# Part of the first MLP product as seven half-size products, with weight sums made by adding DMAs

## The chip, the cores and the metric

The kernel runs on one core of a Trainium2 chip, as one program launched once. The metric is the device time of that program in microseconds (us); smaller is better. TensorE does the matrix products (PE in the profile, with PEld for its weight loads), VectorE the two-operand arithmetic (DVE), ScalarE the copies, casts and functions (ACT), GpSimd some helpers (POOL), and SyncE asks for most of the transfers (SP). The profile calls the sequencers that issue DMAs SPq, ACTq and POOLq.

## The reference

A two-layer encoder on 512 tokens of width 1024. Layer 0 has an attention mixer, layer 1 a retention mixer; each is followed by an MLP with 4096 hidden units. Only the MLP is touched in what it computes:

```python
def _rmsnorm(x, g):
    xf = x.astype(jnp.float32)
    y = xf * lax.rsqrt(jnp.mean(xf * xf, axis=-1, keepdims=True) + RMS_EPS)
    return (y * g.astype(jnp.float32)).astype(x.dtype)

def _mlp(x, norm_g, w1, w2):
    h = _rmsnorm(x, norm_g)
    return jnp.square(jax.nn.relu(h @ w1)) @ w2

def reference(x, ...):
    for layer in range(DEPTH):          # DEPTH = 2
        ...
        x = x + _mlp(x, mlp_norm[layer], w_mlp_in[layer], w_mlp_out[layer])
    return x
```

Here `w1` is 1024 x 4096 and `w2` 4096 x 1024, all in float32.

## The kernel before

**Layout.** The residual lies transposed in SBUF: `xT[d]` holds features 128d to 128d+127 on the partitions and the 512 tokens in a row. `Norm.add` splits each tile, times the gain, into a rounded part and a rest (`xh`, `xl`, of type float32r); the row factor of the norm, `rb` (`norm.rows`), is applied after the product, since it is one number per token. Weights are split in the same way by `load_w`: one DMA on SP brings 512 KB into a `wraw` tile of 128 x 1024 (three buffers), ScalarE writes the rounded part `whi` (line 157), VectorE the rest `wlo` (line 158), two buffers each. A product of two such numbers is three matmuls: hi x hi, hi x lo, lo x hi.

**One projection.** `proj_a` makes 256 output columns for all 512 tokens: for each of 8 row tiles k and each half m of the columns three matmuls with a 128 x 128 weight and a 128 x 512 moving operand (lines 176 to 178), 48 in all, into two PSUM banks (`acc`, four buffers; `aux` is a second group of four). Then `evac` is called for each bank.

**The MLP.** `mlp` runs over four quarters q of the hidden units. In each it calls `proj_a` four times for the first product (c = 0 to 3, 1024 columns of `w1`), and then four times for the second (`w2`, 8 row tiles of the quarter's hidden units, added into `xT` at line 1043). The last quarter of layer 1 uses `store` and `proj_b` in place of the second. In this text a **unit** is 512 columns of the first product, two calls of `proj_a`; there are 8 units in a layer, two in a quarter. The evacuation of one bank (lines 1029 to 1033) is a chain: VectorE `max(ps, 0) * rb`, ScalarE square, ScalarE cast to `hh`, VectorE `hl = h - hh`.

**Order.** The Python order gives priorities; a scheduler at build time then places the instructions of each engine in the order in which it thinks they become ready, and `high_priority` moves the weight splits ahead. On the chip each engine runs its list in that order and waits at semaphores. A tile of a pool with n buffers can be written again when every reader of the tile n turns before it is done; a load that needs it waits on its queue till then.

Besides the MLP the change touches small tiles of the two mixers (`rstd`, `ssq`, `rs`, `lg`, `gn` and others), the `ones` constants and the eight idle matmuls at the start (line 83), `rstd_c` in `cols`, and the tag of the output tile `o` in `store`.

Of the kernel before, what the change touches and what calls it, by code (L numbers as in the profile page):

```python
# [9 lines left out]
F32 = mybir.dt.float32  # L10
F32R = mybir.dt.float32r
AF = mybir.ActivationFunctionType
ALU = mybir.AluOpType
# [19 lines left out]
def hybrid_encoder_kernel(  # L33
# [40 lines left out]
    ones = consts.tile([P, P], F32, name="ones")  # L74
    V.memset(ones, 1.0)
# [6 lines left out]
    for _ in range(8):  # L82
        mm(idle[:, :P], ones, ones, start=True, stop=True)
    ones_r = consts.tile([P, P], F32R, name="ones_r")
    V.tensor_copy(ones_r, ones)
    isl = consts.tile([P, 16], F32, name="isl")
# [7 lines left out]
    V.tensor_scalar(nsink, hb[:, 0:8], -1.0, None, op0=ALU.mult)  # L94

# [245 lines left out]
    def cols(row):  # L341
# [6 lines left out]
        r = stat.tile([P, 16], F32, tag="rstd_c", name="rstd_c")  # L348
        V.tensor_copy(r[:, 0:8], pc[:, 0:8])
        return r  # L350


    def even_mixer(next_norm):
        es = ExitStack()
        pool = es.enter_context(tc.tile_pool(name="even", bufs=1))
        xg = new_xg()
# [43 lines left out]
        rstd = pool.tile([P, 16], F32, name="rstd")[:, :NB]  # L400

        def token_norms():
            ssq = pool.tile([P, 4, NB], F32, name="ssq")
# [14 lines left out]
            v = pool.tile([P, 16], F32, name="ssv")[:, :NB]  # L418
            V.tensor_scalar(v, ssq[:, 0], 1.0 / D, RMS_EPS, op0=ALU.mult, op1=ALU.add)
            rsqrt_small(rstd, v, NB, pool)  # L420
# [5 lines left out]
        class HeadNorm:  # L426
# [5 lines left out]
            def __init__(self, raw, dsts, extra=None):  # L432
# [3 lines left out]
                self.ss = pool.tile([P, NB, 6], F32, tag="ss", bufs=2, name="ss")  # L436
# [10 lines left out]
            def finish(self, order):  # L447
                nh, extra = self.nh, self.extra
                self.rs = pool.tile([P, NB, nh], F32, tag=f"rs{nh}", bufs=2, name="rs")
                v = pool.tile([P, NB, nh], F32, tag=f"sv{nh}", bufs=2, name="sv")  # L450
# [4 lines left out]
                rsqrt_small(flat(self.rs), flat(v), NB * nh, pool)  # L455
# [132 lines left out]
        def small(tag):  # L588
            return pool.tile([P, 4], F32, tag=tag, bufs=4, name=tag)
# [381 lines left out]
    def store(w, hid, pool):  # L971
# [17 lines left out]
        for half in range(2):  # L989

            def ev(t, ps):
                o = pool.tile([P, S], F32, tag="o", bufs=3, name="o")
# [17 lines left out]

    def mlp(layer, norm, on_final, last=False):
        with tc.tile_pool(name=f"mlp{layer}", bufs=1) as pool:
            rb = None
            for q in range(4):
                hid = [
                    (
                        pool.tile([P, S], F32R, tag=f"hh{k}", name="hh"),
                        pool.tile([P, S], F32R, tag=f"hl{k}", name="hl"),
                    )
                    for k in range(8)  # L1020
                ]
                for c in range(4):
# [27 lines left out]
    def odd_mixer(norm, next_norm):  # L1050
# [69 lines left out]
        class Quarter:  # L1120


            def __init__(self, qt):
                self.qt = qt
# [256 lines left out]
```

## Time and profile before

| what | value |
|---|---|
| median of 3 runs | 1368.46 us (1367.3 to 1368.81) |
| the profiled execution, its own time | 1366.27 us |
| its span in the profile | 1364.5 us |
| granted TensorE clock, mean | 0.999 |
| HBM read | 120.43 MB |

The profile is of one execution. Its span runs from the first to the last instruction that it shows; 1.77 us lie around it. Busy times are those of each engine; matmuls overlap, so the time that one takes is longer than the distance to the next one, and it is the distance that counts. The chain that ended last is followed back from the last instruction: at each step it names the instruction that was waited for.

### The profile page before, as it was taken

Reading aid. Unit: us, or ns where it says so; the run is one execution under the profiler, and the core shown is the slowest. Engines: PE = TensorE matmul, PEld = TensorE weight load, DVE = VectorE, ACT = ScalarE, POOL = GpSimd, SP = SyncE. Lnnn points to the kernel's source line nnn. Section 1 sums busy time; section 2 is a strip of 40 time slices with the busy share of each in tenths; the row PEclk is TensorE's granted clock in tenths of the full one; section 3 lists DMA queues with packets and bytes.
Section 4 is the critical chain, followed back from the end, with each engine's and each line's share of the span. In section 5 each row is a group of like instructions: output and inputs, shape, how many; then the busy total and the mean of one; then the engine's idle time right before and its main releaser. Section 6 shows DMA issues by size and latency. Waiting matters only on the chain.

```text
span 1364.5 us, 16240 instructions
## 1 busy us (share of the span) xinstructions
PE 1346.2 (99%) x6218; PEld 1118.4 (82%) x6218; DVE 767.7 (56%) x1228; ACT 591.8 (43%) x1008; POOL 68.1 (5%) x80
## 2 busy tenths in 40 slices
PE   8999999999999999999999999999999999999998
PEld 7889887788888888888888888888888888888887
DVE  6788887634434434576758448547575344343433
ACT  4788775422313323344734445435354133241331
POOL 0223333000000000000000000000000000000000
PEclk9999999999999999999999999999999999999999
DMA  5322322323233233332231331331332333223322
GB/s 168 88 79 84 98 63 85 108 93 93 94 104 96 93 93 105 96 106 62 78 95 47 97 102 47 93 96 53 99 93 93 93 102 99 93 93 96 105 87 84
DMA packets 129502, 124.64 MB, mean 91 GB/s; under 512 B 9472, under 2 KB 122128, under 8 KB 129424
## 3 DMA queue, kind: packets, MB, share of 16 engines
q1 hardware_dynamic: 123648, 120.21, 28.3%
q10 hardware_dynamic: 5744, 3.37, 0.9%
q8 instruction: 49, 0.80, 0.2%
q14 instruction: 29, 0.24, 0.1%
q0 software_dynamic: 32, 0.01, 0.0%
HBM read 120.43 MB, written 3.15 MB: 91 GB/s over the span
## 4 chain that ended last, share of the span: by engine, by line
PE 91%; DVE 4%; ACT 2%; DMA 1%; issue 1%; POOL 0%; ACTq 0%; SPq 0%; DVEq 0%
PE acc L176 22%; PE acc L178 22%; PE acc L177 22%; PE acc L252 4%; PE acc L251 4%; PE acc L253 4%; PE aux L1202 1%; PE aux L1204 1%; PE aux L1203 1%; PE acc L200 1%; PE acc L202 1%; PE acc L201 1%; DVE wlo L158 1%; PE acc L229 1%; PE acc L227 1%
## 5 line engine op out<-in xcount | busy, mean ns | idle before, releaser
L157 ACT CAST whi<-wraw 128x1024 fp32r<-128x1024 f32 (+2 forms) x227 | 230.1, 1014 | 640.1 <-PE acc L177 531.5
L158 DVE TENSOR_TENSOR wlo<-wraw,whi 128x1024 fp32r<-128x1024 f32 (+2 forms) x218 | 261.1, 1198 | 293.3 <-ACT whi L157 292.0
L176 PE MATMUL acc<-xh,whi 128*128 128x512 f32 x784 | 305.4, 390 | 1.4 <-DVE xT L848 1.4
L177 PE MATMUL acc<-xl,whi 128*128 128x512 f32 x784 | 305.3, 389 | 0.3 <-DVE xl L298 0.3
L178 PE MATMUL acc<-xh,wlo 128*128 128x512 f32 x784 | 305.3, 389 | 0.0
L176 PE MATMUL acc<-hh,whi 128*128 128x512 f32 x448 | 176.5, 394 | 0.0
L178 PE MATMUL acc<-hh,wlo 128*128 128x512 f32 x448 | 175.6, 392 | 0.0
L177 PE MATMUL acc<-hl,whi 128*128 128x512 f32 x448 | 173.9, 388 | 0.0
L176 PEld LDWEIGHTS acc<-xh,whi 128*128 128x128 f32 x784 | 147.1, 188 | 32.6 <-DVE xT L848 1.8
L177 PEld LDWEIGHTS acc<-xl,whi 128*128 128x128 f32 x784 | 147.2, 188 | 31.6 <-DVE xl L298 1.0
L178 PEld LDWEIGHTS acc<-xh,wlo 128*128 128x128 f32 x784 | 147.1, 188 | 31.0 <-DVE wlo L158 0.2
L178 PEld LDWEIGHTS acc<-hh,wlo 128*128 128x128 f32 x448 | 84.1, 188 | 19.7
L177 PEld LDWEIGHTS acc<-hl,whi 128*128 128x128 f32 x448 | 84.1, 188 | 18.8
L176 PEld LDWEIGHTS acc<-hh,whi 128*128 128x128 f32 x448 | 84.2, 188 | 16.8
L1029 DVE SCALAR_TENSOR_TENSOR t<-acc,rstd_b 128x512 f32<-128x512 f32 x64 | 43.7, 692 | 77.1 <-PE acc L178 77.0
L1043 DVE TENSOR_TENSOR xT<-xT,acc 128x512 f32<-128x512 f32 x56 | 38.5, 688 | 76.1 <-PE acc L178 76.1
L251 PE MATMUL acc<-whi,xh 128*128 128x512 f32 x160 | 63.4, 396 | 0.0
L252 PE MATMUL acc<-wlo,xh 128*128 128x512 f32 x160 | 62.9, 393 | 0.2 <-DVE wlo L149 0.2
L253 PE MATMUL acc<-whi,xl 128*128 128x512 f32 x160 | 62.3, 390 | 0.0
L201 PE MATMUL acc<-wlo,xh 128*128 128x384 f32 (+1 forms) x160 | 52.6, 329 | 0.0
L200 PE MATMUL acc<-whi,xh 128*128 128x384 f32 (+1 forms) x160 | 52.6, 331 | 0.0
L202 PE MATMUL acc<-whi,xl 128*128 128x384 f32 (+1 forms) x160 | 52.1, 327 | 0.0
(231 smaller groups left out, 1915.4 us busy)
## 6 DMA issues: line engine op xcount, KB each, us to landing
wraw<-in_w_mlp_in_dram SPq DMA_DIRECT2D x64, 512.0 KB
wraw<-in_w_mlp_out_dram SPq DMA_DIRECT2D x64, 512.0 KB
wraw<-in_w_in_o_dram SPq DMA_DIRECT2D x48, 512.0 KB
wraw<-in_w_out_o_dram SPq DMA_DIRECT2D x16, 512.0 KB
wraw<-in_w_in_e_dram SPq DMA_DIRECT2D x48, 128.0 KB
wraw<-in_w_in_e_dram SPq DMA_DIRECT2D x12, 256.0 KB
wraw<-in_w_out_e_dram SPq DMA_DIRECT2D x4, 512.0 KB
wraw<-in_w_out_e_dram SPq DMA_DIRECT2D x8, 256.0 KB
```

Of the source, the lines that this page charges most:

```text
L157: nc.scalar.copy(hu, used)
L158: eng.tensor_tensor(lu, used, hu.bitcast(F32), op=ALU.subtract)
L176: mm(ps[m], hi[:, k % 4, cs], xh, start=k == 0, stop=False)
L177: mm(ps[m], hi[:, k % 4, cs], xl, start=False, stop=False)
L178: mm(ps[m], lo[:, k % 4, cs], xh, start=False, stop=k == nk - 1)
L200: mm(o, lh, hi[:, k, :ncols], start=kb + k == 0, stop=False)
L201: mm(o, lh, lo[:, k, :ncols], start=False, stop=False)
L202: mm(o, ll, hi[:, k, :ncols], start=False, stop=kb + k == KT - 1)
L251: mm(o, lh, hi[:, k, :ncols], start=kb + k == 0, stop=False)
L252: mm(o, lh, lo[:, k, :ncols], start=False, stop=False)
L253: mm(o, ll, hi[:, k, :ncols], start=False, stop=kb + k == KT - 1)
L1029: V.scalar_tensor_tensor(t, ps, 0.0, rb, op0=ALU.max, op1=ALU.mult)
```

## The change

In both layers units 2 to 7 of the first product are made by a class `Seven`, and units 0 and 1 as before, with `proj_a`. `Seven` cuts the 512 columns of a unit into two halves of 256, the 1024 rows of the weight into even and odd row tiles, and the 512 tokens into two halves of 256. That gives 2 x 2 blocks on both sides, and the four result blocks come from seven products of blocks instead of eight, in Winograd's form of Strassen's scheme. Each of the seven is 4 row tiles x 2 column tiles x 3 matmuls, with a 128 x 256 moving operand.

- **Input side.** `combine` makes for each pair of row tiles four sums of blocks (U1, U2, T3, T4) and splits them, four times per layer, in units 0 and 1; they serve all six units.
- **Weight side.** A unit needs seven 128 x 1024 blocks: A11, A12, A22 as loaded; S1 = A21 + A22 and S3 = A21 + A11, each loaded by a DMA on SP and completed by a second DMA on GpSimd that adds into the tile (the signs of the scheme are taken up elsewhere, so that all are sums); S2 = S1 + A11 and S4 = S2 + A12 by VectorE, S4 in S2's place. Three tiles each for loaded blocks (`sraw`), sums (`ssum`), rounded parts (`shi`) and rests (`slo`).
- **Order.** The blocks are split two products ahead of their use (`prepare`). The loads of the next unit stand in the program ahead of the fourth product of this one.
- **Output side.** The seven products run through three banks, `a` (four of the products, accumulating), `b` (one) and `c` (two). ScalarE copies partial results out (`keep`), VectorE adds (`add`), and `evac` ends each of the four result blocks with the same chain of four instructions; two blocks are negated and use `min` for `max`.
- **Around it.** The hidden units lie in tiles of 128 x 2 x 512, `t` and `h` become one tile squared in place, the small tiles of the mixers move into pools of their own, `ones` is written as float32r and used for the idle matmuls, `rstd_c` becomes a constant tile, and a filler of 80 words per partition is added.

```diff
-    ones = consts.tile([P, P], F32, name="ones")
-    V.memset(ones, 1.0)
+    ones_r = consts.tile([P, P], F32R, name="ones_r")
+    V.memset(ones_r[:].bitcast(F32), 1.0)
...
-        mm(idle[:, :P], ones, ones, start=True, stop=True)
-    ones_r = consts.tile([P, P], F32R, name="ones_r")
-    V.tensor_copy(ones_r, ones)
+        mm(idle[:, :P], ones_r, ones_r, start=True, stop=True)
...
+    class Seven:
+        BLOCKS = ("A11", "A12", "S2", "S1", "S3", "S4", "A22")
+        INPUTS = ("B11", "B21", "U2", "U1", "T3", "B22", "T4")
...
+        def combine(self, i):
+            pool, norm = self.pool, self.norm
+            y = []
+            for m in range(2):
+                d = 2 * i + m
+                t = pool.tile([P, S], F32, tag="s", bufs=5, name="y")
+                act(t, xT[d], AF.Copy, scale=gv[:, norm.vec + d : norm.vec + d + 1])
+                y.append(t)
+            b11, b12 = y[0][:, :256], y[0][:, 256:]
+            b21, b22 = y[1][:, :256], y[1][:, 256:]
+            c = pool.tile([P, 4, 256], F32, tag="slo", bufs=3, name="c")
+            V.tensor_tensor(c[:, 0], b11, b12, op=ALU.subtract)
+            V.scalar_tensor_tensor(c[:, 1], c[:, 0], -1.0, b22, op0=ALU.mult, op1=ALU.subtract)
+            V.tensor_tensor(c[:, 2], b22, b12, op=ALU.subtract)
+            V.scalar_tensor_tensor(c[:, 3], c[:, 1], -1.0, b21, op0=ALU.mult, op1=ALU.subtract)
+            h = pool.tile([P, 4, 256], F32R, tag=f"uh{i}", name="uh")
+            l = pool.tile([P, 4, 256], F32R, tag=f"ul{i}", name="ul")
+            nc.scalar.copy(h, c)
+            V.tensor_tensor(l, c, h[:].bitcast(F32), op=ALU.subtract)
...
+        def load(self, u, names=("S1", "S3", "A11", "A12", "A22")):
+            r = self.raw.setdefault(u, {})
+            for name in names:
+                tag = "ssum" if name[0] == "S" else "sraw"
+                r[name] = self.pool.tile([P, 4, 256], F32, tag=tag, bufs=3, name=tag)
+                if name[0] == "S":
+                    nc.sync.dma_start(r[name], self.source(u, "A21"))
+                    second = self.source(u, "A22" if name == "S1" else "A11")
+                    G.dma_start(r[name], second, accum_op=ALU.add)
+                else:
+                    nc.sync.dma_start(r[name], self.source(u, name))
+
+        def split(self, u, j):
+            name, r = self.BLOCKS[j], self.raw[u]
+            if name == "S2":
+                r[name] = self.pool.tile([P, 4, 256], F32, tag="ssum", bufs=3, name="ssum")
+                V.tensor_tensor(r[name], r["S1"], r["A11"], op=ALU.add)
+            if name == "S4":
+                r[name] = r["S2"]
+                V.tensor_tensor(r[name], r["S2"], r["A12"], op=ALU.add)
+            h = self.pool.tile([P, 4, 256], F32R, tag="shi", bufs=3, name="shi")
+            l = self.pool.tile([P, 4, 256], F32R, tag="slo", bufs=3, name="slo")
+            nc.scalar.copy(h, r[name])
+            V.tensor_tensor(l, r[name], h[:].bitcast(F32), op=ALU.subtract)
+            self.parts[u, j] = (h, l)
...
+        def product(self, u, j, ps, start):
+            h, l = self.parts.pop((u, j))
+            for m in range(2):
+                o = ps[:, m * 256 : (m + 1) * 256]
+                cs = slice(m * P, (m + 1) * P)
+                for i in range(4):
+                    bh, bl = self.ins[i][self.INPUTS[j]]
+                    first = start and m == 0 and i == 0
+                    mm(o, h[:, i, cs], bh, start=first, stop=False, skip_group_check=True)
+                    mm(o, h[:, i, cs], bl, start=False, stop=False, skip_group_check=True)
+                    mm(o, l[:, i, cs], bh, start=False, stop=i == 3, skip_group_check=True)
+
+        def run(self, u, evac):
...
+            def keep(ps):
+                s = pool.tile([P, S], F32, tag="s", bufs=5, name="s")
+                nc.scalar.copy(s, ps)
+                return s
+
+            def add(s, ps):
+                V.tensor_tensor(s, s, ps, op=ALU.add)
+                return s
+
+            a, b, c = acc(), aux(), acc()
+            self.prepare(1)
+            self.product(u, 0, a, True)
+            s1 = keep(a)
+            self.prepare(1)
+            self.product(u, 1, b, True)
+            evac(0, 0, add(s1, b), 1)
+            self.prepare(1)
+            self.product(u, 2, a, False)
+            s2 = keep(a)
+            self.prepare(1)
+            if u < 7:
+                self.load(u + 1)
+            self.product(u, 3, c, True)
+            s5 = keep(c)
+            self.prepare(1)
+            self.product(u, 4, a, False)
+            evac(1, 1, add(s5, keep(a)), -1)
+            self.prepare(1)
+            self.product(u, 5, c, False)
+            evac(0, 1, add(s2, c), 1)
+            self.prepare(1)
+            self.product(u, 6, a, False)
+            evac(1, 0, a, -1)
...
     def mlp(layer, norm, on_final, last=False):
...
+            seven.queue = [(u, j) for u in range(2, 8) for j in range(7)]
...
+                for c in range(2):
+                    u = 2 * q + c
+                    if u < 2:
...
+                            proj_a(w1[layer], 0, 8, u * 512 + c2 * 256, norm.xg, ev)
+                            seven.combine(2 * u + c2)
+                            if (u, c2) == (0, 1):
+                                seven.load(2, ("A11", "A12"))
+                            if (u, c2) == (1, 0):
+                                seven.load(2, ("S1", "S3"))
+                                seven.prepare(2)
+                        if u == 1:
+                            seven.load(2, ("A22",))
+                        continue
+
+                    def evac(fb, half, ps, sign):
+                        hs = slice(half * 256, (half + 1) * 256)
+                        h, l = (x[:, :, hs] for x in blocks[2 * c + fb])
+                        t = ps if sign > 0 or half else tmp()
+                        two = lambda v: v[:].rearrange("p (m t) -> p m t", m=2)
+                        V.scalar_tensor_tensor(
+                            two(t),
+                            two(ps),
+                            0.0,
+                            rb[:, hs].unsqueeze(1).to_broadcast([P, 2, 256]),
+                            op0=ALU.max if sign > 0 else ALU.min,
+                            op1=ALU.mult,
+                        )
+                        act(t, t, AF.Square)
+                        nc.scalar.copy(h, two(t))
+                        V.tensor_tensor(l, two(t), h.bitcast(F32), op=ALU.subtract)
+
+                    seven.run(u, evac)
```

More of the change, by code (lines that the diff above doesn't have):

```diff
@@ L1022, in mlp @@
[L1022 to L1035 removed]
+                blocks = [
+                    [
+                        pool.tile([P, 2, S], F32R, tag=f"h{x}{k}", name=f"h{x}")
+                        for x in ("h", "l")
+                    ]
+                    for k in range(4)
+                ]
```

107 lines of the change are left out of this document (68 added, 39 removed).

## The prediction, on record before the result

> **What bounds the kernel now.** I read the page's first part, then the chain that ended last, then the table of stretches, for one quarter's first product (two units, four projections) and for a second product.
>
> ```profile
> span 1364.5 us, 16240 instructions
> PE 1346.2 (99%) x6218; PEld 1118.4 (82%) x6218; DVE 767.7 (56%) x1228; ACT 591.8 (43%) x1008; POOL 68.1 (5%) x80
> PE 91%; DVE 4%; ACT 2%; DMA 1%; issue 1%; POOL 0%; ACTq 0%; SPq 0%; DVEq 0%
> core 0: us, PE busy (x) PEld busy (x) DVE busy (x) ACT busy (x) POOL busy (x), PEclk, DMA share, GB/s
> 409.38:452.96 43.58, 43.58 (x193) 36.04 (x192) 19.18 (x22) 14.67 (x20) 0.00 (x0) 1.00 0.31 97
> ...
> 365.43:409.38 43.95, 43.95 (x193) 36.06 (x192) 16.60 (x18) 10.51 (x12) 0.00 (x0) 1.00 0.30 95
> ```
>
> TensorE is the bound: 91% of the chain is its own work. In the row before the last a pair of units takes 43.58 us, TensorE is busy for all of it at full clock (1.00), VectorE for 19.18, ScalarE for 14.67. Such a pair is 4 x 48 = 192 matmuls, so one 512-wide matmul costs 43.58 / 192 = 0.2270 us. Nothing else is late in this stage; only fewer or cheaper matmuls can shorten it. Twelve of the sixteen units, six pairs, are changed.
>
> **The matmuls.** A changed unit has 7 x 24 = 168 matmuls of 256 columns instead of 96 of 512. In columns that is 7/8. What a 256-wide one costs is seen in the attention mixer, where a run of them, each with a new weight, goes without a break. The timeline of PE, first and last of 40 in a row:
>
> ```profile
> 154.63 0.28 PE L200 MATMUL acc<-whi,xh 128*128 128x256 f32 x1
> ...
> 159.29 0.28 PE L200 MATMUL acc<-whi,xh 128*128 128x256 f32 x1
> ```
>
> 39 steps in 4.66 us: 0.1195 us each, more than half of 0.2270 (0.1135). So narrow matmuls lose part of the eighth. A pair becomes 336 x 0.1195 = 40.15 us, against 43.58: **3.43 us per pair, 20.6 us over six pairs** (a full eighth would have been 32.7). One product takes 24 x 0.1195 = 2.87 us, a unit 20.08. The bound from the other side: there is no shorter step in the trace at this width, so 20.6 is the most.
>
> **What VectorE and ScalarE must now do in that time.** The groups of instructions with shapes kept apart:
>
> ```profile
> L157 ACT CAST whi<-wraw 128x1024 fp32r<-128x1024 f32 x199 | 209.4, 1052 | 630.6 <-PE acc L177 529.4 <-PE acc L253 68.3 <-issue 31.1
> L1031 ACT ACTIVATE h<-t 128x512 f32<-128x512 f32 x64 | 36.6, 620 | 0.0
> L1032 ACT CAST hh<-h 128x512 fp32r<-128x512 f32 x64 | 36.0, 610 | 0.0
> L1206 ACT COPY of<-aux 128x512 f32<-128x512 f32 x16 | 9.1, 585 | 10.5 <-PE aux L1204 10.4
> L297 ACT ACTIVATE xh<-xT,gv 128x512 fp32r<-128x512 f32 x24 | 17.2, 716 | 6.4 <-DVE xT L848 6.4
> L158 DVE TENSOR_TENSOR wlo<-wraw,whi 128x1024 fp32r<-128x1024 f32 x197 | 242.1, 1229 | 288.9 <-ACT whi L157 288.4
> L1029 DVE SCALAR_TENSOR_TENSOR t<-acc,rstd_b 128x512 f32<-128x512 f32 x64 | 43.7, 692 | 77.1 <-PE acc L178 77.0
> L1033 DVE TENSOR_TENSOR hl<-h,hh 128x512 fp32r<-128x512 f32 x64 | 41.4, 688 | 10.6 <-ACT hh L1032 10.6
> L995 DVE TENSOR_TENSOR o<-acc,rows 128x256 f32<-128x256 f32 x2 | 0.8, 420 | 0.7 <-PE acc L253 0.7
> ```
>
> ScalarE per unit: 7 casts of 1.05, 4 copies out of PSUM of 0.585, 4 x (0.62 + 0.61) = 14.6 us of 20.08, 73%. VectorE per unit: 7 rests and the two sums S2 and S4, 9 x 1.23 = 11.1; 3 adds, 4 max/min and 4 rests of 128x512, 11 x 0.69 = 7.6; together 18.7 us, 93%. That looks tight, but in a packed stretch the next instruction starts before the last one's time is up:
>
> ```profile
> 996.25 1.22 DVE L158 TENSOR_TENSOR wlo<-wraw,whi 128x1024 fp32r<-128x1024 f32 x1
> 997.38 0.75 DVE L298 SCALAR_TENSOR_TENSOR xl<-xT,gv,xh 128x512 fp32r<-128x512 f32 x1
> 998.05 0.69 DVE L317 TENSOR_TENSOR sqsum<-sqsum,sq 128x512 f32<-128x512 f32 x1
> 998.65 0.75 DVE L298 SCALAR_TENSOR_TENSOR xl<-xT,gv,xh 128x512 fp32r<-128x512 f32 x1
> ```
>
> From start to start: 1.13 for the large form, 0.60 for the small. So VectorE needs 9 x 1.13 + 11 x 0.60 = 16.8 us per unit, 84%, and has 3.3 us to spare. Whether it can use them depends on hand-offs: in the chain max, square, cast, rest VectorE waits 1.23 us for ScalarE in between, and after S2 and S4 1.05 us for the cast, unless other work is ready. The order before shows that it is filled:
>
> ```profile
> 507.86 1.37 DVE L1029 SCALAR_TENSOR_TENSOR t<-acc,rstd_b 128x512 f32<-128x512 f32 x2 [2.67 <-PE acc L178]
> 509.39 1.23 DVE L158 TENSOR_TENSOR wlo<-wraw,whi 128x1024 fp32r<-128x1024 f32 x1 [0.17 <-ACT whi L157]
> 510.95 1.29 DVE L1033 TENSOR_TENSOR hl<-h,hh 128x512 fp32r<-128x512 f32 x2 [0.33 <-ACT hh L1032]
> ```
>
> A weight's rest stands between the max and the rests of the hidden tile, and only 0.17 and 0.33 us are idle.
>
> **Where it is late.** The work is uneven. The four result blocks end after products 1, 4, 5 and 6 (counted from 0). From the end of product 4 to the end of the next unit's product 0, three products' time or 8.6 us, VectorE has three splits and S2 (4 x 1.13) and three chains (8 x 0.60): 9.3 us. It ends 0.7 us behind, and S2's split is what product 2 of the next unit needs. In the first unit of a pair S2 can be made during the second product before it, where VectorE is mostly free; in the second it can't. After product 1 there is slack again, since a split may start when the product three before it is done. I take **0.8 us of stall per pair, 4.8 us in all**; bounds: nothing, and, if none of the hand-offs is filled (4 x 1.23 + 2 x 1.05 = 7.0 us), VectorE's 23.8 us per unit, which is longer than before.
>
> The first waits of the new output side cost nothing: product 2 waits until ScalarE has copied `a`, which has product 1's 2.87 us for 0.585 us; products 4, 5 and 6 likewise. Behind such a copy on ScalarE stand casts that are due two products later. At the pair's end the last chain (0.69 + 0.62 + 0.61 + 0.69 = 2.6 us) is needed by the second product's row tile 6, 36 matmuls or 8.2 us later.
>
> **The weight sums.** The loads before never waited for data: SP waited for tiles. The DMA rows, and two small transfers of the chain:
>
> ```profile
> SPq L136 <- DVE wlo L158: 1043.1, 195, 23.3
> q1 hardware_dynamic: 123648, 120.21, 28.3%
> hb<-in_heads_dram POOLq DMA_DIRECT2D x1, 12.0 KB, 6.0
> 1.24 0.70 POOL L79 DMA_DIRECT2D hb<-in_heads_dram  x1 [0.80 <-POOLq L1366]
> 65.08 2.06 DMA scr_v<-raw
> ```
>
> 120.21 MB in 28.3% of 1364.5 us is 311 GB/s when the queue's engines work. A block (0.524 MB) then takes 1.69 us of transfer, and 3.75 with the 2.06 us that a small one takes. A unit now moves 7 blocks, 3.67 MB: 11.8 us of 20.08, if adding costs no more than copying. That fits. The traffic grows by 12 x 3 blocks, 18.9 MB.
>
> Adding DMAs are not in the trace. The only transfer of GpSimd took 6.0 us from issue to landing for 12 KB, at the busy start. Lowest price: a load's 3.75 us; upwards the trace gives no end. I take the nearest row, 6.0 plus 1.65 us for the remaining bytes: 7.65. The Trainium skill, "DMA: Bandwidth & Descriptors", section "Anatomy of one DMA — SWDGE (gpsimd) path", gives about 2.0 us plus bytes at 436 GB/s for a plain one, by which it would be an estimate of 3.2 us; no run here shows it.
>
> When must it be there? SP and GpSimd run ahead of the program's place as far as tiles come free. S1's tile is free when its rest is done: not before the end of product 0 plus 1.05 + 1.23 = 5.15 us into the unit, at the latest at the start of product 3, 8.6 us. Loaded 3.75 us later, added 7.65 us later: at 16.6 to 20.0 us. S2 must begin 1.23 + 1.05 + 1.23 us ahead of product 2 of the next unit (25.8 us): at 22.3. **It is in time by 2.3 to 5.7 us.** S3's adding DMA stands behind S1's on GpSimd's queue; one after the other they end at 24.2 to 27.7, and product 4 needs its split begun at 29.3. A11 and A12 are plain loads behind them on SP, with some 3 us to spare. The first unit of a pair has the 44 us of a second product ahead of it. So I cost the transfers at nothing, up to about 9 us per adding DMA; beyond that see the rivals.
>
> **The rest.** `combine` adds two per unit in units 0 and 1: ScalarE 2 x (2 x 0.716 + 1.05) = 5.0 us, VectorE 2 x (4 x 0.42 + 1.23) = 5.8 us, in 21.8 us in which VectorE was busy for under half. The second buffer of `whi`/`wlo` covers 24 matmuls, 5.4 us. Nothing; at most 2 us per layer. The idle matmuls at the start get shorter:
>
> ```profile
> 1.05 3.78 PE L83 MATMUL aux<-ones 128*128 128x128 f32 x16 [1.05 <-DVE ones L75]
> 9.25 0.87 PE L372 MATMUL aux<-ident,qk 128*128 128x128 f32 x4 [3.56 <-DMA qk<-in_x_dram]
> ```
>
> TensorE waits for the input until 9.25 us in any case. If the clock rises later for it, 1 to 2 us; I take nothing. Small tiles in other pools issue the same instructions: nothing.
>
> **The sum.** 1366.27 us (profiled execution: span and 1.77 us around it) - 20.6 + 4.8 = 1350.5 us. The median of the runs, 1368.46, lies 2.2 us above the profiled execution, so on its scale: **1352.7 us**.
>
> **Rivals.**
>
> 1. *VectorE's hand-offs stay open.* It becomes the bound when its idle time per changed unit exceeds 3.3 us, and the gain is used up at 21.79 - 16.8 = 5.0 us. Half of the 7.0 us open: 20.3 us per unit, still 12 x 1.5 = 18 us gained, the stalls among it; four fifths open, 22.4 us per unit, +7 us. A variant is contention with GpSimd. VectorE's L476 shows it:
>
> ```profile
> L476 DVE TENSOR_TENSOR qn<-raw,rs x10: 415/857/1352, 41.0 to 183.0; 128x256 f32<-128x256 f32 x10
> ```
>
> One form, 415 to 1352 ns, in the stage where GpSimd works. If each of the two adding DMAs of a unit stretched one instruction by 0.94 us, VectorE would need 18.7 us; still under 20.08, but stalls grow by a us or two per pair: about 1362. Against it: the descriptors took GpSimd 0.70 us in the row above. The Trainium skill, "SBUF — State Buffer", section "Who interferes with whom", has a VectorE instruction with two SBUF inputs blocked by a GpSimd one that reads SBUF; every rest here has two. L476 agrees, but no run here shows it for a DMA issue.
>
> 2. *The adding DMAs are late (the slower side).* The point is S3: its two adding DMAs in a row must fit between about 10.6 us (middle of the above) and 29.3, so 9.3 us each. At 12 us each S3 comes at 34.6, 5.3 us late, once per pair: +32 us against -20.6, so 1380. VectorE and ScalarE run in order, so a sum that waits also holds the copies behind it. For it: 6.0 us for only 12 KB; the addition has to read the tile as well; the loads of A11 and A12 run at the same time. Against it: 311 GB/s of capacity, of which 97 were used in this stage.
>
> 3. *The change doesn't do what it says.* The loads are asked for when tiles come free, not four products ahead; if S1's rest falls behind by a product, S1 is 2.9 us later, in time or barely late: 1353 to 1362.
>
> **Chances.** The forecast, 1348 to 1358: 0.60. VectorE or the asking partly in the way (rivals 1 and 3), 1358 to 1365.7: 0.14; within 0.2% of 1368.46 (2.7 us, about what a measurement of this kernel can tell from no change): 0.07. Slower, nearly all by rival 2: 0.19. That makes 0.74, 0.07 and 0.19. The range goes from 1346 (a us or two for a better start) to 1378, which leaves out some 0.16 above, the worse part of rival 2.
>
> **What would show it.** Right: in a pair's stretch TensorE steps by 0.1195 us, the pair takes 40 to 41.5 us, VectorE is busy 34 to 38 us of it, and the largest wait of TensorE there is at product 2 of the second unit, for a rest. Wrong: adding DMAs of over 9 us and TensorE waiting behind S2 or S3; VectorE with gaps of 1 us after each max; a step above 0.1195; a stretched form of VectorE beside GpSimd's issues. The second products (44 us) should not change.

## The result, and the profile after

The changed kernel takes **1386.59 us** (median of 4 runs, 1384.3 to 1389.1) against 1367.88 us before (median of 4, 1367.3 to 1368.81): **1.0139 times the time, 95% interval 1.0120 to 1.0157**. The forecast was 1352.7 us, the range 1346 to 1378. It is slower by 1.4%, and the time lies outside the range. Three executions on record, of 1870.49, 1916.94 and 5662.93 us, were disturbed and enter no figure below.

The page of the changed kernel: span, busy times, the chain that ended last by engine and by line, and the rows of the adding DMAs (their issue on GpSimd; the time from issue to landing).

```profile
span 1387.3 us, 18219 instructions
...
PE 1334.2 (96%) x7074; PEld 1149.9 (83%) x7074; DVE 872.3 (63%) x1363; ACT 674.3 (49%) x1116; POOL 98.5 (7%) x104
...
PE 77%; DVE 10%; DMA 6%; issue 3%; ACT 3%; POOL 0%; ACTq 0%; SPq 0%; DVEq 0%; POOLq 0%
...
L1074 POOL DMA_DIRECT2D ssum<-in_w_mlp_in_dram x24 | 30.9, 1290 | 979.9 <-DVE wlo L159 429.8
...
ssum<-in_w_mlp_in_dram POOLq DMA_DIRECT2D x24, 512.0 KB, 7.2
```

TensorE's own work is 77% of the chain, where it was 91%; VectorE has gone from 4% to 10% and transfers from 1% to 6%. TensorE was busy for 1346.2 us before and is for 1334.2 now: the arithmetic has become less, and the span is 22.8 us longer all the same. So TensorE waits.

Where it waits is read from the table of stretches of the changed kernel, layer 0: pair of units, second product, and so on three times. (After the times: length, then busy time and instructions of PE, PEld, DVE, ACT, POOL, then the granted clock, DMA share and GB/s.)

```profile
322.40:364.60 42.20, 40.67 (x337) 40.43 (x336) 26.37 (x30) 24.03 (x32) 5.14 (x4) 1.00 0.63 146
364.60:416.50 51.90, 46.23 (x195) 37.43 (x194) 23.70 (x27) 11.73 (x14) 0.00 (x0) 0.93 0.39 105
416.50:459.10 42.60, 40.65 (x338) 40.40 (x337) 26.32 (x30) 24.02 (x32) 5.13 (x4) 1.00 0.62 145
459.10:511.40 52.30, 46.73 (x195) 37.79 (x194) 23.70 (x27) 11.72 (x14) 0.00 (x0) 0.93 0.38 104
511.40:554.10 42.70, 40.70 (x338) 40.45 (x337) 29.61 (x35) 23.95 (x34) 2.56 (x2) 1.00 0.35 75
554.10:597.60 43.50, 43.50 (x194) 36.04 (x194) 22.02 (x28) 16.06 (x22) 0.00 (x0) 1.00 0.27 85
```

A pair takes 42.2 to 42.7 us, with TensorE busy for 40.7: the matmuls got cheaper as forecast, and some 2 us of each pair are idle. The surprise is in the second products, whose code is the same. Before, they took 43.95 us. The two that are followed by another pair take 51.9 and 52.3 us, with a granted clock of 0.93; the third, after the layer's last unit, takes 43.5 at full clock.

The account, from the starts of TensorE's stages in both traces: the six pairs together 5.7 us shorter (20.6 were forecast); the four second products followed by another pair 28.4 us longer (7.9, 8.4, 2.9, 9.2); the starts of the two MLPs 0.7 and 1.2 us later; the other second products and the end 1.8 us shorter. That is 22.8 us, the difference of the spans.

The waits of the changed kernel (who waited, for whom: us in all, times, longest):

```profile
DVE ssum L1083 <- DMA ssum<-in_w_mlp_in_dram: 65.6, 10, 9.1
...
PE acc L177 <- ACT hh L1211: 16.4, 4, 5.8
...
PE acc L1109 <- DVE slo L1090: 10.6, 6, 2.0
...
PE acc L178 <- DVE hl L1212: 4.4, 4, 1.3
```

L1083 is the sum S2 = S1 + A11, made by VectorE. It waits 65.6 us in ten places for an adding DMA. TensorE waits six times for a rest (`slo`), once in each pair, and four times, at the start of a second product, for hidden tiles (`hh`, `hl`). How one comes from the other is seen in the timeline. The first fence has VectorE, with one row each of SP and GpSimd, in the first pair of layer 0; unit 2 begins at 322.6. (Start, duration, engine, line; in brackets how long the engine sat idle before it, and what ended that.)

```profile
327.86 3.68 SPq L1072 DMA_DIRECT2D ssum<-in_w_mlp_in_dram  x2
...
332.38 1.23 DVE L1090 TENSOR_TENSOR slo<-ssum,shi 128x1024 fp32r<-128x1024 f32 x1 [0.31 <-ACT shi L1089]
...
332.56 1.30 POOL L1074 DMA_DIRECT2D ssum<-in_w_mlp_in_dram  x1 [88.24 <-DVE hl L1212]
...
339.36 1.23 DVE L1083 TENSOR_TENSOR ssum<-ssum,sraw 128x1024 f32<-128x1024 f32 x1 [5.76 <-DMA ssum<-in_w_mlp_in_dram]
340.50 2.35 DVE L1090 TENSOR_TENSOR slo<-sraw,shi 128x1024 fp32r<-128x1024 f32 x2
342.77 0.68 DVE L1121 TENSOR_TENSOR s<-s 128x512 f32<-128x512 f32 x1
...
366.54 1.23 DVE L1083 TENSOR_TENSOR ssum<-ssum,sraw 128x1024 f32<-128x1024 f32 x1 [7.88 <-DMA ssum<-in_w_mlp_in_dram]
367.68 1.22 DVE L1090 TENSOR_TENSOR slo<-sraw,shi 128x1024 fp32r<-128x1024 f32 x1
368.81 0.69 DVE L1121 TENSOR_TENSOR s<-s 128x512 f32<-128x512 f32 x1
369.53 0.69 DVE L1202 SCALAR_TENSOR_TENSOR s<-s,rstd_b 128x512 f32<-128x512 f32 x1
```

S1's load for the next unit is asked for 5.3 us into the unit and its adding DMA at 10.0 us; S2 starts 16.8 us in. But VectorE was ready for S2 at 333.6, 11.0 us in, since that is where S2 stands in its order. It stood idle for 5.76 us, and behind it in the same order stand the rest of this unit's last block, A22, and its adds and maxes, which had nothing to do with the next unit, with the rests of the next unit's A11 and A12 between them. In the second unit of the pair the same happens with the S2 of the pair after: 7.88 us.

The same two places on TensorE:

```profile
339.97 0.28 PE L1108 MATMUL acc<-ul,shi 128*128 128x256 f32 x1
341.77 0.38 PE L1109 MATMUL acc<-uh,slo 128*128 128x256 f32 x1 [1.53 <-DVE slo L1090]
...
374.99 0.79 PE L177 MATMUL acc<-hh,whi 128*128 128x512 f32 x1 [4.64 <-ACT hh L1211]
376.81 0.79 PE L178 MATMUL acc<-hl,whi 128*128 128x512 f32 x1 [1.03 <-DVE hl L1212]
...
378.25 0.63 PE L178 MATMUL acc<-hl,whi 128*128 128x512 f32 x1
378.68 0.63 PE L179 MATMUL acc<-hh,wlo 128*128 128x512 f32 x1
...
380.98 0.40 PE L179 MATMUL acc<-hh,wlo 128*128 128x512 f32 x1
381.22 0.39 PE L177 MATMUL acc<-hh,whi 128*128 128x512 f32 x1
```

In the pair, product 6 waits for the rest of A22, made right behind S2. In the second product TensorE reaches the row tile that needs the unit's last result blocks; their adds and maxes stood behind S2 till 367.7, then came the squares and casts. It waits 4.64 us, does one matmul, waits again, and from then on steps by 0.43 us instead of 0.23, until 380.4: the granted clock has halved. So a second product pays three times: the wait, the second wait, and the slow matmuls.

### The profile page after: what moved, and what is told of

It reads as the page before. It is cut to its first block, busy times and chain, and to the rows that moved or that the text cites. A ratio compares the mean times of both kernels' runs of the same rounds, so it can differ in the third digit from the quotient of the medians.

```text
span 1387.3 us, 18219 instructions
## 1 busy us (share of the span) xinstructions
PE 1334.2 (96%) x7074; PEld 1149.9 (83%) x7074; DVE 872.3 (63%) x1363; ACT 674.3 (49%) x1116; POOL 98.5 (7%) x104
## 3 DMA queue, kind: packets, MB, share of 16 engines
HBM read 139.30 MB, written 3.15 MB: 103 GB/s over the span
## 4 chain that ended last, share of the span: by engine, by line
PE 77%; DVE 10%; DMA 6%; issue 3%; ACT 3%; POOL 0%; ACTq 0%; SPq 0%; DVEq 0%; POOLq 0%
PE acc L178 15%; PE acc L179 15%; PE acc L177 15%; DMA ssum<-in_w_mlp_in_dram 5%; PE acc L252 4%; PE acc L253 4%; PE acc L254 4%; PE acc L1109 3%; PE acc L1107 3%; PE acc L1108 3%; DVE slo L1090 2%; PE aux L1382 1%; PE aux L1383 1%; PE aux L1384 1%; DVE wlo L159 1%
## 5 line engine op out<-in xcount | busy, mean ns | idle before, releaser
L177 PE MATMUL acc<-hh,whi 128*128 128x512 f32 x448 | 177.8, 397 | 16.4 <-ACT hh L1211 16.4
L177 PE MATMUL acc<-xh,whi 128*128 128x512 f32 x400 | 156.4, 391 | 2.4 <-DVE xT L849 1.9
L179 PE MATMUL acc<-xh,wlo 128*128 128x512 f32 x400 | 156.4, 391 | 0.9 <-DVE wlo L159 0.9
L178 PE MATMUL acc<-xl,whi 128*128 128x512 f32 x400 | 156.4, 391 | 0.0
L1109 PE MATMUL acc<-uh,slo 128*128 128x256 f32 x384 | 109.8, 286 | 10.6 <-DVE slo L1090 10.6
L1107 PE MATMUL acc<-uh,shi 128*128 128x256 f32 x384 | 109.4, 285 | 0.0
L1108 PE MATMUL acc<-ul,shi 128*128 128x256 f32 x384 | 109.1, 284 | 0.0
L179 PEld LDWEIGHTS acc<-xh,wlo 128*128 128x128 f32 x400 | 75.5, 189 | 17.3 <-DVE wlo L159 1.4
L178 PEld LDWEIGHTS acc<-xl,whi 128*128 128x128 f32 x400 | 75.4, 188 | 15.6
L1109 PEld LDWEIGHTS acc<-uh,slo 128*128 128x128 f32 x384 | 74.2, 193 | 11.8 <-DVE slo L1090 11.8
L1108 PEld LDWEIGHTS acc<-ul,shi 128*128 128x128 f32 x384 | 74.2, 193 | 0.0
L1107 PEld LDWEIGHTS acc<-uh,shi 128*128 128x128 f32 x384 | 74.0, 193 | 0.0
```

Of the source, the lines that this page charges most:

```text
L177: mm(ps[m], hi[:, k % 4, cs], xh, start=k == 0, stop=False)
L178: mm(ps[m], hi[:, k % 4, cs], xl, start=False, stop=False)
L179: mm(ps[m], lo[:, k % 4, cs], xh, start=False, stop=k == nk - 1)
L1107: mm(o, h[:, i, cs], bh, start=first, stop=False, skip_group_check=True)
L1108: mm(o, h[:, i, cs], bl, start=False, stop=False, skip_group_check=True)
L1109: mm(o, l[:, i, cs], bh, start=False, stop=i == 3, skip_group_check=True)
```

## The experiments

The first theory (A in the expectations): S2's *place* in VectorE's order costs the time; the adding DMAs are as fast as they need be. The rivals: the adding DMAs themselves are too slow or disturb VectorE, so that no place helps; and the second products suffer from something of their own, the new tiles of the hidden units or another placement in SBUF. All times below are medians; ratios are to the kernel before on the same chip, with 95% intervals.

**1. S2 held back (e1_hold_s2).** The sum may not be placed ahead of the last max of the unit before it; nothing else changes. Unit 2 has no such unit before it and isn't held.

```diff
             if name == "S2":
-                V.tensor_tensor(r[name], r["S1"], r["A11"], op=ALU.add)
+                s2 = V.tensor_tensor(r[name], r["S1"], r["A11"], op=ALU.add)
+                if self.held is not None:
+                    after(s2.ins, self.held.ins)
...
-                        V.scalar_tensor_tensor(
+                        seven.held = V.scalar_tensor_tensor(
```

> The sum S2 of each next unit (except unit 2) is put behind the last max of the unit before it on VectorE; nothing else is changed. Theory A (the sum stands too early in VectorE's order, waits there 6 to 9 us for the adding DMA, and holds all work behind it): the waits of S2 for the DMA go to under 1 us each, the four slow second products fall from 47 to 53 us to 43.5, the clock stays whole in them, pairs take 40.5 to 41.5 us, and the kernel takes 1350 us (1345 to 1356). Rival B (the adding DMA as such is too slow for the work behind it): the same waits come back later, at product 2 of the second unit of a pair, and the time stays above 1368. Rival C (VectorE's hand-offs are the bound): pairs stay at 42 us or more without any wait for a DMA, 1358 to 1366.

Measured: **1345.76 us** (1344.16 to 1347.58), ratio 0.9839 (0.9825 to 0.9852). One edit of order takes 40.8 us off the changed kernel. The page of this run, then its stretches (first pair and second product of layer 0), then the rows of S2 and of the rests in its groups:

```profile
span 1345.8 us, 18247 instructions
...
PE 1321.6 (98%) x7074; PEld 1142.7 (85%) x7074; DVE 873.9 (65%) x1363; ACT 676.9 (50%) x1116; POOL 98.5 (7%) x104
...
PE 88%; DVE 6%; ACT 2%; DMA 2%; issue 1%; POOL 0%; ACTq 0%; SPq 0%; DVEq 0%; POOLq 0%
...
ssum<-in_w_mlp_in_dram POOLq DMA_DIRECT2D x24, 512.0 KB, 8.6
```

```profile
324.60:364.90 40.30, 40.30 (x337) 40.29 (x336) 31.02 (x36) 25.48 (x34) 5.15 (x4) 1.00 0.66 154
364.90:408.50 43.60, 43.60 (x195) 36.09 (x194) 19.59 (x22) 10.80 (x13) 0.00 (x0) 1.00 0.45 124
```

```profile
L1093 DVE TENSOR_TENSOR slo<-ssum,shi 128x1024 fp32r<-128x1024 f32 x48 | 58.7, 1222 | 14.3 <-ACT shi L1092 14.3
...
L1084 DVE TENSOR_TENSOR ssum<-ssum,sraw 128x1024 f32<-128x1024 f32 x12 | 14.6, 1219 | 7.4 <-issue 5.0 <-DMA ssum<-in_w_mlp_in_dram 2.4
```

The pair takes 40.3 us with TensorE busy throughout, the second product 43.6 at full clock. The adding DMAs are no faster here (8.6 us, 7.2 in the changed kernel) and read the same 139.30 MB with the others; VectorE's busy time is the same (873.9 and 872.3 us). What went is the wait: S2 waits 2.4 us for the DMA, where it waited 65.6. The timeline of VectorE in this run shows S2 where it does no harm, behind the unit's last max, 21.6 us after the unit's beginning at 324.6:

```profile
345.57 0.68 DVE L1205 SCALAR_TENSOR_TENSOR s<-acc,rstd_b 128x512 f32<-128x512 f32 x1
346.17 1.22 DVE L1084 TENSOR_TENSOR ssum<-ssum,sraw 128x1024 f32<-128x1024 f32 x1
```

Side by side, VectorE's lists of the two kernels differ in nothing but the ten held sums and, beside each, two rests of a hidden tile that now stand ahead of two other instructions. TensorE's list is the same; ScalarE's moved a little with the sums.

**2. No adding DMAs (e2_no_adding).** S1 and S3 keep only their first block; S2 stands where the scheduler puts it. The second block of both sums is left out.

```diff
                 if name[0] == "S":
                     nc.sync.dma_start(r[name], self.source(u, "A21"))
-                    second = self.source(u, "A22" if name == "S1" else "A11")
-                    G.dma_start(r[name], second, accum_op=ALU.add)
```

> The adding DMAs are left out (S1 and S3 hold the first block alone, so the sums lack one block), all else as in the changed kernel. Theory A and rival B both expect the wait of S2 to end with the plain load, some 7 us earlier: about 1352. Rival C expects no change of the pairs beyond the waits: over 1358 and pairs of 42 us.

Measured: 1344.0 us (one run). Pairs of 40.3, second products of 43.5 us; the time is 8 us below what was expected. The order differs a little from that of the changed kernel, so this isn't quite the same list with an earlier arrival. But in the first pair S2 stands where it stood, 11.05 us into the unit, and starts there without a wait; in all it waits 1.5 us. So with the data there in time the place does no harm. Theory A and rival B expected the same of this run, and it doesn't decide between them; run 1 does. Pairs and second products take as long as in run 1, so the adding DMAs with their 12.6 MB and GpSimd's issues cost nothing that shows in these stages. The 1.8 us between the totals are less than run 1's own spread.

**3. The sums on VectorE (e3_vector_sums).** S1 = A21 + A22 and S3 by VectorE in place of the adding DMAs, with S1 held as S2 was in run 1.

```diff
-                    second = self.source(u, "A22" if name == "S1" else "A11")
-                    G.dma_start(r[name], second, accum_op=ALU.add)
...
-                V.tensor_tensor(r[name], r["S1"], r["A11"], op=ALU.add)
+                s1 = V.tensor_tensor(r["S1"], r["S1"], r["A22"], op=ALU.add)
+                s2 = V.tensor_tensor(r[name], r["S1"], r["A11"], op=ALU.add)
+                if self.held is not None:
+                    after(s1.ins, self.held.ins)
+                V.tensor_tensor(r["S3"], r["S3"], r["A11"], op=ALU.add)
```

> S1 and S3 are added by VectorE instead of by DMA, and S1's and S2's sums stand behind the last max of the unit before, as in the run that holds S2. VectorE gets 2 x 1.13 us more per unit, 19.1 of 20.1 us. Theory A: no DMA chain, but a VectorE that is nearly full: pairs of 41 to 43 us, 1352 to 1362. Rival B: faster than the run that only holds S2. Rival C: 1366 or more.

Measured: 1348.66 us, 0.9861 (0.9846 to 0.9876); pairs of some 41 us, one of 42. That is better than the 1352 to 1362 expected: VectorE almost has room for two more sums per unit. Adding by DMA, once placed rightly, is worth about 3 us against it (1345.76); the two intervals still overlap. Whether the 3 us are want of room isn't shown: the sum S3 was not held here, and its trace shows it waiting 20.0 us in eleven places for its plain load, 3.1 us at most.

**4. One half of the holding each (e13_hold_even, e14_hold_odd).** Run 1 removed two losses at once. Each pair is an even and an odd unit. The S2 of an odd unit (3, 5, 7) is made during the even one, inside a pair; that of units 4 and 6 at the end of a pair, ahead of a second product.

```diff
-                if self.held is not None:
+                if self.held is not None and u % 2 == 0:
```

> S2 is held behind the last max of the unit before only for units 4 and 6, whose wait stands at the end of a pair, ahead of a second product. Theory A: the four slow second products (51.9, 52.3, 46.9 and 53.2 us in the changed kernel) fall to 43.4, 30.7 us in all, and the pairs keep the stall of 1.5 to 3.5 us that the S2 of the odd unit makes: 1356 (1352 to 1360). If the stall within a pair was the main loss, 1372 or more.

Measured: 1364.20 us (median of four), 0.9966 (0.9952 to 0.9980). The other half has `u % 2 == 1`:

> S2 is held only for units 3, 5 and 7, whose wait stands inside a pair. Theory A: the pairs fall to 40.3 to 41 us (up to 14 us in all), the four second products stay at 47 to 53 us with the clock at 0.93 or so: 1373 (1368 to 1378). The two savings of this run and of the one that holds the even units add up to that of the run that holds all.

Measured: 1374.94 us, 1.0049 (1.0033 to 1.0066). First pair and second product of layer 0, first with only even units held, then with only odd ones:

```profile
324.50:366.90 42.40, 40.69 (x338) 40.45 (x337) 30.84 (x36) 25.20 (x34) 5.14 (x4) 1.00 0.63 146
366.90:410.40 43.50, 43.50 (x194) 36.04 (x194) 19.42 (x22) 10.75 (x12) 0.00 (x0) 1.00 0.45 125
```

```profile
324.10:364.30 40.20, 40.20 (x337) 40.19 (x335) 26.45 (x30) 24.31 (x32) 5.15 (x4) 1.00 0.66 155
364.30:413.90 49.60, 45.45 (x195) 36.89 (x194) 23.51 (x27) 11.87 (x14) 0.00 (x0) 0.97 0.39 109
```

The two losses come apart cleanly. With the even units held all second products take 43.5 us, and the pairs keep their stalls; with the odd ones held all pairs take 40.2 to 40.4 us, and the second products that are followed by another pair stay at 49.6 to 51.0 with a lowered clock. So each loss belongs to one S2, the one that stands ahead of it. The medians don't add up fully: 22.4 and 11.7 us below the changed kernel, together 34.0, where holding both gives 40.8. In the profiled executions the stages themselves do: pairs and second products together are 27.7 us shorter than in the changed kernel with the even units held, 16.3 with the odd ones, 43.9 with both. What doesn't add up lies outside of them or between executions; the four of the changed kernel alone spread over 4.8 us. The first run came out above what was expected of it. Its pairs take 258.1 us in all, 2.3 more than in the changed kernel (255.8): the clock was halved for 3.4 us in two of them, 44.1 and 44.3 us long, and in one of the changed kernel's, 43.8 us. And the start of its first MLP ends some 2 us later, as it does in run 1; why is open.

**5. Holding further (e5_hold_all_s2, e12_hold_middle).** The first holds unit 2's S2 too, behind the last max of unit 1. The second holds every S2 behind an earlier max of the unit, that of the block ending after product 4; unit 2's as in the first.

```diff
-                                V.scalar_tensor_tensor(
+                                seven.held = V.scalar_tensor_tensor(
                                     t, ps, 0.0, rb,
```

> As the run that holds S2, and the S2 of unit 2 too stands behind the last max of unit 1 (before, it stood ahead of the norm's work at the start of each MLP). Theory A: the start of each MLP loses its wait of 1.4 to 2.7 us: 1342 to 1344, against 1345.8 for the run that holds the others alone. If the late starts have another cause: 1345.8.

Measured: 1344.57 us (median of four), 0.9832 (0.9819 to 0.9846). In the profiled executions the starts of the MLPs are 1.7 and 2.1 us shorter than in run 1, but the times of the two versions overlap and can't be told apart.

```diff
-                        seven.held = V.scalar_tensor_tensor(
+                        m = V.scalar_tensor_tensor(
...
+                        if (fb, half) == (1, 1):
+                            seven.held = m
```

> As the run that holds every S2, but behind the max after product 4 of the unit before (some 17 us into the unit) instead of after product 6 (some 21 us). S1 lands 17 to 19 us into the unit. Theory A: S2 waits 0 to 2 us there, mostly hidden: 1343 to 1350, and if the place did not matter by time of landing but only by what stands behind it, over 1355.

Measured: 1344.33 us, 0.9830 (0.9816 to 0.9843). Pairs and second products are as in run 1, and S2 waits 0.6 us in all. Either place will do, this one or the unit's end; all three versions beat the kernel before by 1.6 to 1.7%, and the changed kernel by more.

**6. The second products' own gain.** In all of these the undisturbed second product takes 43.5 us, 0.45 less than before, though its code is the same: a matmul steps by 0.2267 us, before by 0.2290. Three runs look for the cause. The kernel before with the new 128x2x512 tiles for the hidden units:

```diff
-                hid = [
-                    (
-                        pool.tile([P, S], F32R, tag=f"hh{k}", name="hh"),
-                        pool.tile([P, S], F32R, tag=f"hl{k}", name="hl"),
-                    )
-                    for k in range(8)
-                ]
+                blocks = [
+                    [
+                        pool.tile([P, 2, S], F32R, tag=f"h{x}{k}", name=f"h{x}")
+                        for x in ("h", "l")
+                    ]
+                    for k in range(4)
+                ]
+                hid = [(h[:, m], l[:, m]) for h, l in blocks for m in range(2)]
```

> The kernel before, with one part of the change: the hidden units lie in tiles of 128 x 2 x 512 instead of 128 x 512. The undisturbed second products of the changed kernel step by 0.2267 us where those of before step by 0.2290. If that comes from the tiles, the eight second products give 7 x 0.44 us: 1365 against 1368 (0.2% faster). If it comes from the work beside it, nothing changes.

Measured: 1367.71 us, 0.9998 (0.9990 to 1.0007), step 0.2290: the tiles' shape isn't it. The version of e5_hold_all_s2 without the filler of 80 words:

```diff
-    consts.tile([P, 80], F32, name="filler")
```

> As the run that holds every S2, without the filler of 80 words per partition, so that all later tiles lie 320 bytes lower. The second products step by 0.2267 us in all changed kernels and by 0.2290 in the kernel before and in the one with block tiles. If the placement of tiles in SBUF sets that step, it goes to 0.229 or so here and the time rises by some 4 us; if not, no change.

Measured: 1343.58 us, 0.9827 (0.9813 to 0.9840), step still 0.2267: nor the filler. The kernel before with the changed constants alone (`ones` gone, `isl` smaller, `rstd_c` a constant, the filler):

```diff
-    ones = consts.tile([P, P], F32, name="ones")
-    V.memset(ones, 1.0)
+    ones_r = consts.tile([P, P], F32R, name="ones_r")
+    V.memset(ones_r[:].bitcast(F32), 1.0)
...
-    isl = consts.tile([P, 16], F32, name="isl")
+    isl = consts.tile([P, 8], F32, name="isl")
...
+    rstd_c = consts.tile([P, 8], F32, name="rstd_c")
+    consts.tile([P, 80], F32, name="filler")
...
-        r = stat.tile([P, 16], F32, tag="rstd_c", name="rstd_c")
-        V.tensor_copy(r[:, 0:8], pc[:, 0:8])
-        return r
+        V.tensor_copy(rstd_c, pc[:, 0:8])
+        return rstd_c
```

> The kernel before with the changed kernel's constants alone (float32r ones for the idle matmuls, a constant tile for rstd_c, the filler). If the placement sets the step of the second products, they step by 0.2267 instead of 0.2290 us and the time is 1364 to 1365 (0.25 to 0.3% faster); the idle matmuls alone are expected to do nothing. If not, 1367.8.

Measured: 1364.85 us, 0.9980 (0.9971 to 0.9989), second products at 0.2267. So this small edit of the change is worth 2.7 us by itself. It changes where all later tiles lie in SBUF, and little else that these products see, so their place is the likely cause; no run moves the tiles and nothing else to this effect, and which relation of addresses would decide is open. The trace of the kernel before has one more sign: the two matmuls of a group that read `hh` step by 0.2317 and 0.2294 us, the one that reads `hl` by 0.2258; with the constants alone all three step by 0.226 to 0.227.

## Why the prediction was wrong

**The step that failed** is "S2 must begin 1.23 + 1.05 + 1.23 us ahead of product 2 of the next unit (25.8 us): at 22.3. It is in time by 2.3 to 5.7 us." The arrival was right: forecast for 16.6 to 20.0 us into the unit, it came at 16.8 to 17.3 in the first units of the pairs. But it was compared with the time at which the *result* is due, and VectorE waits for its operands at the time at which the instruction stands next in its list, 11.0 us into the unit. The transfer was in time for the matmuls, and 5.7 to 6.2 us late for the list. At the end of a pair the forecast saw no danger ("The first unit of a pair has the 44 us of a second product ahead of it"); there VectorE came to S2 14.2 to 14.3 us into the unit, the data 19.2 to 23.2 us in, and this is the place that cost most. The text says, in rival 2, that a sum that waits holds what stands behind it, yet tied that to a late S3 and to adding DMAs of over 9.3 us. None was needed: with 7.2 us in the median, below the 7.65 assumed, the time came out at the far side. So the sign of rival 2 came true and its trigger didn't; its 1380 us is near 1386.59 by chance.

**What stood behind the waiting sum** wasn't followed to its end either. Adds, maxes and rests of the hidden units late by several us reach the second product, which the text costed as unchanged ("should not change"). That is the larger part, 28.4 us, and it comes from two effects in a row: the wait (16.4 + 4.4 us), and then a stretch at half clock, to which some 9 us are left (an estimate: the four take 30.0 us more than four undisturbed ones). The last chain was given 2.6 us and 8.2 us until it is needed, a margin of 5.6; the wait of 7.88 us is longer. But the margin was itself too large: in the fourth place S2 waited only 4.86 us, and the second product still took 2.9 us more. Behind S2 stand not one chain but two rests, two adds and three maxes.

**What was right.** The narrow matmul: 0.1195 us a step forecast, 0.1200 measured; a pair 40.15 forecast, 40.3 measured with S2 held. Of the 20.6 us to be gained 19.6 are there. VectorE's room: it keeps pace in every held version, so hand-offs (rival 1) are not the bound; it is busy for 31.0 us of a held pair, less than the 34 to 38 named, as only 36 of the pair's 40 instructions fall into it. Contention with GpSimd, rival 1's variant: the issue of an adding DMA keeps GpSimd busy for 1.29 us (0.70 assumed), and the rests take 1222 ns in the mean, 1229 before; no stretching. Traffic: run 2, without the second blocks, has pairs no shorter than run 1. Rival 3, late asking: the load was asked for 5.3 us in, as worked out.

**Two terms that were mis-sized**, seen once S2 is held: the stall of 4.8 us isn't there (the pairs run at 40.3), and the constants, costed at nothing, bring 2.7 us. 1352.7 - 4.8 - 2.7 = 1345.2, and the version with every S2 held takes 1344.57. That the rest comes out even is in part luck: the pairs gain a us less than forecast, and the sum started from 1368.46, 0.6 above the median of 1367.88.

The price of an adding DMA was open in the forecast. The Trainium skill, "DMA: Bandwidth & Descriptors", section "Anatomy of one DMA — SWDGE (gpsimd) path", gave an estimate of 3.2 us for a plain transfer of this size; the adding one took 7.2 us in the changed kernel and 8.6 in the held one. By the estimate from the Trainium skill S2 would have been ready some 4 us earlier, at about 12.8 us, and still behind its place at 11.0.

Open: why the scheduler placed S2 there, and why the start of the first MLP is up to 2 us longer in the versions that leave unit 2's S2 unheld.

## What to carry to other kernels

For each new instruction that needs a late transfer, read its *place* in its engine's list, not the time when its result is due: an engine that runs in order waits at that place, and the price is the work behind it. Where a build-time scheduler writes the list, pin such an instruction behind the last one that must not wait; here that one edge, for ten sums, turned +1.4% into -1.6%. And follow a delay on to the next stage: missing operands ahead of a dense stretch of matmuls also cost clock, here where they left TensorE idle for half of a 3.4 us step or more.

## What the runs showed of the hardware

**The clock.** In the changed kernel TensorE waits 4.64 us at the start of a second product, does a single matmul, waits 1.03 us, and then steps by 0.43 us instead of 0.23 until 380.4; the mean granted clock of that 51.9 us stretch is 0.93. Three of the four disturbed second products go so. The fourth kept its clock. Three rows of PE's timeline in the changed kernel, each a wait: in the second pair of layer 0, in the first pair of layer 1, and in that fourth second product. Then rows of its table of stretches, cut where the clock can change (see below): from the wait of 4.64 us on, around the wait of 1.95 us, and around that of 1.77 us.

```profile
436.25 0.39 PE L1109 MATMUL acc<-uh,slo 128*128 128x256 f32 x1 [1.95 <-DVE slo L1090]
...
1126.83 0.38 PE L1109 MATMUL acc<-uh,slo 128*128 128x256 f32 x1 [1.77 <-DVE slo L1090]
...
1158.28 0.50 PE L177 MATMUL acc<-hh,whi 128*128 128x512 f32 x1 [1.43 <-ACT hh L1211]
```

```profile
370.40:373.81 3.41, 0.00 (x0) 0.00 (x0) 3.41 (x6) 2.67 (x5) 0.00 (x0) 1.00 0.48 142
373.81:377.22 3.41, 1.20 (x2) 0.70 (x3) 3.38 (x4) 2.59 (x5) 0.00 (x0) 0.50 0.00 0
377.22:380.64 3.42, 3.42 (x9) 2.65 (x9) 1.28 (x2) 0.00 (x0) 0.00 (x0) 0.50 0.73 196
...
431.84:435.25 3.41, 2.46 (x21) 2.25 (x19) 1.42 (x2) 1.83 (x3) 0.00 (x0) 1.00 1.13 162
435.25:438.66 3.41, 2.42 (x20) 2.42 (x21) 3.38 (x5) 0.00 (x0) 0.00 (x0) 1.00 0.39 86
438.66:442.08 3.42, 3.42 (x30) 3.42 (x30) 3.42 (x5) 2.66 (x4) 0.00 (x0) 1.00 0.77 240
...
1124.74:1128.16 3.42, 1.65 (x14) 1.45 (x13) 3.42 (x4) 1.04 (x1) 0.00 (x0) 1.00 0.96 143
1128.16:1131.57 3.41, 3.41 (x19) 3.41 (x18) 3.38 (x6) 2.15 (x3) 0.00 (x0) 0.50 0.88 251
```

The wait of 1.77 us is followed by 3.41 us at half clock, in the only pair of this trace where that happened; the longer one of 1.95 us and that of 1.43 us cost no clock. So the length of a wait alone doesn't decide, but its position does. In each trace the granted clock changes only at times that lie a multiple of 3.41 us apart. Cut along this grid, from the start of the first MLP (about 215 us) to the end of the last second product, the twelve traces show one rule: a step at full clock in which TensorE was idle for 1.72 us or more was followed by one at half clock, all 13 times, and a step with 1.71 us or less never was. The wait of 1.77 us lies in one step, which leaves 1.65 us busy; that of 1.95 us lies across two, with 2.46 and 2.42 us busy. The Trainium skill, "TensorE: Matmul & The Clock Gate", section "Part 1: The HAM clock gate (the "warmup" mystery)", tells of a halving after an idle window of about 3.4 us, counted by windows that run freely. The grid of 3.41 us and the long waits agree with it; the wait of 1.77 us fills only half of such a window, and the clock was halved all the same.

**Placement.** The same matmuls with the same operands step by 0.2290 us, or by 0.2267 us after a change of small constants that moves the later tiles in SBUF: 1% of a second product, and 2.7 us of the kernel. That the place of the tiles is the cause is likely and not shown.

**The adding DMA.** 512 KB added into SBUF took 7.2 us in the median from issue to landing in the changed kernel and 8.6 in run 1, and 1.29 us of GpSimd for the issue.
